# Which tiles a Strassen down-projection leaves plain, when its residuals are loaded, and in which order two 64x64 merges are issued

## The chip, the core and the metric

The kernel runs on one core of a Trainium2 chip, as one program. The metric is the device time of one execution in microseconds (us). The median of the runs is what a kernel is judged by. A separate profiled execution gives the trace from which the profile's lines come.

In the text PE is TensorE (matrix products), DVE is VectorE, ACT is ScalarE, POOL is GpSimd, and SP is SyncE, whose queue issues most of the transfers between the chip's main memory and the on-chip memory.

## The reference, cut to what matters

Two layers of a hybrid encoder over 1040 tokens (16 meta tokens and 1024 others), model width 1024, in float32. Each layer is a mixer followed by a SwiGLU block, with RMSNorm ahead of both and residual additions behind both. The mixer joins a bidirectional gated delta rule (4 heads of 128, chunks of 64) and a short gated convolution. What the change touches is this:

```python
# SwiGLU, D_FF = 2816 = 22 tiles of 128
gate, up = jnp.split(h @ w_gate_up, 2, axis=-1)
h = h + (jax.nn.silu(gate) * up) @ w_down
# gated delta rule, in each chunk and direction: a unit triangular system
A = M + jnp.eye(CHUNK)            # M strictly triangular
u = triangular_solve(A, vb); w = triangular_solve(A, kb * jnp.exp(G)[..., None])
```

The kernel works the chunks in blocks of 128 tokens and needs the inverse of one 128x128 unit triangular matrix for each block, head and direction: 8 blocks and 4 heads, 32 inverses a direction (a ninth block of 16 meta tokens is handled by itself).

## The kernel before

Activations lie transposed: 128 channels on the partitions, the tokens along the free dimension. Every float32 operand of a large product is split into a high part `hi`, rounded to the format that PE multiplies fast, and a remainder `lo`, and a product is three matmuls: hi by hi, hi by lo, lo by hi. The split is one ACT instruction (`hi`) and one DVE or POOL instruction (`lo`).

The program is written with a tile framework. It tracks dependencies between tiles, and at build time it places the instructions of each engine into one fixed order by priority and by a simulated timeline; on the chip each engine, and SP's queue of loads, then works through its list in that order. A helper `after(ins, prev)` adds a dependency by hand, `low(f)` issues PE work at the priority of the dense products, and three lists `jobs`, `jobs2`, `jobs3` hold small pieces of work: after each dense group (the products of one output tile over a third of the tokens or so) `dense` takes one piece from each list.

**The inverses.** `invert(d)` returns, for direction d, a list of steps that goes into `jobs3`, one step between two dense groups. A 128x128 inverse is put together from four 32x32 inverses, which DVE has worked out by substitution. `first`, `second` and `third` (lines 560, 568, 578) join 32x32 blocks into 64x64 ones. Then come the two products that join the two 64x64 halves, F_ and S_: `fourth` (line 589) multiplies a block of P_ (rows F_, columns S_) with X64 (rows F_) and puts the result, negated by ACT, into X64 (rows S_); `fifth` (line 594) multiplies that with P_ (rows S_) and puts the result into P_ (rows F_, columns S_). In each direction both are done for 32 matrices in four groups of eight, numbered by `qh`. The steps are `fourth` for groups 0 and 1, `fifth` for 0 and 1, `fourth` for 2 and 3, `fifth` for 2 and 3: four steps of 16 matmuls. The direction d = 0 uses two PSUM banks of the tag "f", d = 1 two of the tag "b". After the inverses of both directions comes the scan over the chunks, which runs between the remaining dense groups.

**Gate and up.** A loop over the 22 f tiles computes both projections by a Strassen scheme of seven products and ends with the row `uv = silu(gate) * up` of that tile, which SP writes to the scratch array `ad[f]` in main memory (line 1335). For some f, DVE also forms the difference of the row's two token halves (line 1337), which goes to the scratch array `td`.

**Down.** The down projection contracts over the 22 f tiles. Four of them (NF = 4) are taken plainly; the other 18 go through a Strassen scheme with seven products, in the order P2, P5, P3, P1, P6, P7, P4 (`SEVEN`). The 18 tiles form two halves `fh` of NP = 9 tiles, the output's 8 tiles two halves `dh` of 4, and the tokens two halves `z`: z = 0 is the two middle quarters, z = 1 the outer two. `UNITS` lists 84 units (product, block b of three tiles, output tile m): 12 units a product. A unit's matmuls (lines 1401 to 1403) are 18 of 260 columns in layer 0 and 9 of 512 columns in layer 1. Ahead of each unit the list `under[u]` issues what later units need:

- `w_unit(u + 5)`: the weight slice of the unit five further on, loaded by `a_load` or taken from sums of slices (`s_sum`), and split (lines 1181, 1182);
- `t_pair(t)`: the row for the right-hand operand, three for a block. It is loaded from `ad` by `b_load` (line 1200) or from `td` (line 1215) and split (lines 1223, 1224). P2 and P3 read the second half of the tiles (`fh` = 1), P1 and P7 the first;
- from unit 60 on, `plain_row`: the rows of the four plain tiles.

In the blocks b = 1 of P2, P5, P3 and P7 the loop also loads the residual half (`hd` to `hr`, line 1382) to which the product of this output tile is added at the end of its block b = 2, four units later. `hr` lies where two operands of gate and up were. The first slices and rows are issued while the last f tile is still being worked on (`down_begins`). After the units the four plain tiles are multiplied by an ordinary `dense`; in layer 1 their weights are split earlier (`last_weights`).

The plain tiles are f = 0 to 3, and the halves are f = 4 to 12 and 13 to 21:

```python
f0 = NF + NP * fh + 3 * (n // 4)                                        # a_load
dma(to.rearrange("p (g e) -> p g e", g=2), half(ad[NF + NP * fh + i][:, o0:L], z))   # b_load
if NF <= f < NF + NP:                                                    # gate and up
    ...
    dma(td[f - NF], gv[:, 0:NB])
```

Of the kernel before, what the change touches and what calls it, by code (L numbers as in the profile page):

```python
# [10 lines left out]
AF = mybir.ActivationFunctionType  # L11
# [6 lines left out]
L = 1040  # L18
H = 4
HD = 128  # L20
FT = 22
# [16 lines left out]
NF = 4  # L38
# [4 lines left out]
def trunk(ctx: ExitStack, tc: tile.TileContext, xT, w_in, w_ba, w_out, w_gu, w_dn,  # L43
# [235 lines left out]
    for l in range(DEPTH):  # L279
# [257 lines left out]
        def invert(d):  # L537
# [46 lines left out]

            F_, S_ = (slice(0, 64), slice(64, 128)) if d == 0 else (slice(64, 128), slice(0, 64))

            def fourth(qh):
                ps = fb(64)
                low(lambda: [mm(ps[S_, q, :], P_[F_, 8 * qh + q, S_], X64[F_, 8 * qh + q, :], start=True, stop=True) for q in range(8)])
                act(out=X64[S_, 8 * qh:8 * qh + 8, :], in_=ps[S_], func=AF.Copy, scale=-1.0)  # L590

            def fifth(qh):
                ps = fb(64)
                low(lambda: [mm(ps[F_, q, :], X64[S_, 8 * qh + q, :], P_[S_, 8 * qh + q, S_], start=True, stop=True) for q in range(8)])
                act(out=P_[F_, 8 * qh:8 * qh + 8, S_], in_=ps[F_], func=AF.Copy)

            return [first, second, third] + [lambda f=f, q=q: [f(q), f(q + 1)] for q in (0, 2) for f in (fourth, fifth)]

        l2s = {}

# [516 lines left out]
            return big(tag, dt).rearrange("p a b -> p (a b)")  # L1117

        def a_load(to, dh, fh, n):
            f0 = NF + NP * fh + 3 * (n // 4)  # L1120
            dma(to.rearrange("p (k e) -> p k e", k=3), w_dn[l, 4 * dh + n % 4, :, f0:f0 + 3, :])
            return to

# [73 lines left out]

        def b_load(fh, z, i):
            to = b_room()
            dma(to.rearrange("p (g e) -> p g e", g=2), half(ad[NF + NP * fh + i][:, o0:L], z))  # L1200
            return to

        def t_slot(t):
# [53 lines left out]
        for f in range(FT):  # L1257
# [75 lines left out]
            act(out=gv, in_=gv, func=AF.Silu)  # L1333
            tt(out=uv, in0=uv, in1=gv, op=ALU.mult)
            dma(ad[f][:, o0:L], uv)
            if NF <= f < NF + NP:
                tt(out=gv[:, 0:NB].rearrange("p (g e) -> p g e", g=2), in0=half(uv, 1), in1=half(uv, 0), op=ALU.subtract)
                dma(td[f - NF], gv[:, 0:NB])
            s_under(f)


# [6 lines left out]
        def plain_row(f):  # L1348

            u = b_room(2)  # L1350
            dma(u, ad[f][:, o0:L])
            lo = row(X[1], F32R, 3) if f < 3 else row(X[1] + "f", F32R)
            act(out=ax[:, f, o0:L], in_=u, func=AF.Copy)
            tt(out=lo[:, o0:L], in0=u, in1=ax[:, f, o0:L].bitcast(F32), op=ALU.subtract)
            rest.append((ax[:, f, :], lo))
# [5 lines left out]
        def last_weights(m):  # L1361
            if not fin_w:
                fin_w.append(flat(Y[0][2], F32R)[:, 0:4096].rearrange("p (m k e) -> p m k e", m=8, k=4))
                rows = [row(Y[1], F32R, 3) for _ in range(3)] + [row(Y[1] + "f", F32R)]
                fin_w.append([r[:, 512 * q:512 * q + 512].rearrange("p (k e) -> p k e", k=4) for r in rows for q in range(2)])
            hi, lo = fin_w[0][:, m], fin_w[1][m]
            wsplit(w_dn[l, m, :, 0:NF, :], hi, lo, raw4(("raw", "ck2")[m % 2]))
            wds.append([(hi[:, k], lo[:, k]) for k in range(4)])


# [2 lines left out]

        FIRST = {"P2": (0, 0), "P5": (1, 1), "P3": (0, 1), "P7": (1, 0)}
        bks = {}
        for i in range(NF):
            under[60 + 3 * i].append(lambda i=i: plain_row(i))
        for u, (p, b, m) in enumerate(UNITS):
            if b == 1 and p in FIRST:
                dh, z = FIRST[p]  # L1380
                q = 4 * dh + m
                dma(half(hr[q][:, o0:L], z), half(hd[q][:, o0:L], z))
            for fn in under[u]:
                fn()
            if last and u == 77:
                for q in range(KT):
                    last_weights(q)
            if not last and u >= len(UNITS) - 2:
                pre["dn", u - len(UNITS) + 2] = wload(w_dn[l, u - len(UNITS) + 2, :, 0:NF, :], NF)
            if p in ("P2", "P5", "P1") and b == 0:  # L1390
                for j in range(NJ):
                    bks[m, j] = pbank()
# [1 line left out]
            for j in range(NJ):  # L1394
                ps = bks[m, j]
                cs = slice(CW * j, CW * j + CW)
                for k in range(3):
                    th, tl = t_slot(3 * (u // 4) + k)
                    st = p in ("P2", "P5", "P1") and b == 0 and k == 0
                    en = b == NBK - 1 and k == 2  # L1400
                    mm(ps[:, :CW], wh[:, k, :], th[:, cs], start=st, stop=False, skip_group_check=True)  # L1401
                    mm(ps[:, :CW], wh[:, k, :], tl[:, cs], start=False, stop=False, skip_group_check=True)  # L1402
                    mm(ps[:, :CW], wl[:, k, :], th[:, cs], start=False, stop=en, skip_group_check=True)  # L1403
                if b == NBK - 1:
                    dh, z, op = TO[p]
                    h = part(hr[4 * dh + m], z, j)
                    tt(out=h, in0=pin(ps), in1=h, op=op)
# [4 lines left out]
        if not last:  # L1412
            for m in range(KT):
                then = next_norm(m, x[m], par[:, (l + 1) * P_L + P_N1 + m:(l + 1) * P_L + P_N1 + m + 1], ss)
                dense(pre.pop(("dn", m)) if m < 2 else wload(w_dn[l, m, :, 0:NF, :], NF), rest, chunks, add_h(m, then), pwide)
                dma(hd[m], hr[m])
        else:
            for (n0, n1) in FIN:
# [85 lines left out]
```

## Time and profile before

| What | Value |
|---|---|
| median of 3 runs | 2575.36 us (2570.45 to 2576.59) |
| the profiled execution | 2574.08 us, of which the trace's span is 2572.3 us |
| mean granted TensorE clock | 0.987 |
| PE busy | 2493.8 us, 97% of the span |
| DVE, ACT, POOL busy | 1722.1, 1046.3, 246.3 us |
| moved by DMA | 359.99 MB, mean 140 GB/s |
| Units of Down in layer 0, first to last start | 1073.3 to 1266.2 us |
| Units of Down in layer 1, first to last start | 2322.3 to 2506.7 us |
| merges (lines 589, 594) in layer 0, first to last start | 245.8 to 264.5 us and 318.5 to 338.4 us |
| merges in layer 1, first to last start | 1540.0 to 1559.6 us and 1616.7 to 1636.6 us |

Times in the trace are us from the span's start. "PE pf<-P,whi" is PE writing a PSUM tile of the tag "f" from operands in the tiles named P and whi; a tile's name here is that of its memory slot, so one slot serves many arrays over the run. A line "A <- B: 10.1, 1, 10.1" in the list of waits says that A stood idle until B, for 10.1 us in all, once, at most 10.1 us. In a timeline the columns are start, duration, engine, line, operation, tiles, shape and count, and in brackets the idle time ahead and what ended it. A matmul's duration overlaps the next one's: the pace is the distance between starts. A line of windows gives the window, its length, the busy time of PE, its weight loads, DVE, ACT and POOL (number of instructions in brackets), the granted clock, and the DMA engines' share and rate in GB/s.

### The profile page before, as it was taken

The page shows a single profiled execution, that of the slowest core. Times are in us where ns is not written, and L with a number is a line of the kernel's source. Part 1 is how long each engine was busy: PE and PEld are TensorE (multiplying, and loading weights), DVE is VectorE, ACT ScalarE, POOL GpSimd, SP SyncE. Part 2 cuts the span into 40 slices and gives each one's busy share as a digit, 9 for nine tenths or more (in the row PEclk, how much of TensorE's full clock was granted, in tenths as well). Part 3 has the DMA queues.
Part 4 walks back from the last instruction along what each step waited for, and adds up shares of the span by engine and source line. Part 5 has one row for each costly group of instructions (what it writes and reads, how often), then busy time and mean ns, then how long its engine had stood idle before and what let it go on. Part 6 is the DMA issues. An engine that isn't in the chain of part 4 may idle for free.

```text
span 2572.3 us, 44715 instructions
## 1 busy us (share of the span) xinstructions
PE 2493.8 (97%) x17442; PEld 2285.1 (89%) x17442; DVE 1722.1 (67%) x3055; ACT 1046.3 (41%) x1933; POOL 246.3 (10%) x264
## 2 busy tenths in 40 slices
PE   8989999999999999989999989999999999999997
PEld 6989999999999999989998878999888888887786
DVE  4678523549877777778656785235698767768866
ACT  5564323426333333434445633323453333334444
POOL 2041212200000000000011302222000000000002
PEclk9999999999999999999999999999999999999998
DMA  3458355524432222663323573456344222238431
GB/s 124 125 166 269 117 174 165 180 73 148 145 110 90 90 93 79 234 208 119 93 93 125 184 243 126 139 178 208 105 143 145 97 94 90 86 108 300 150 114 66
DMA packets 213567, 359.99 MB, mean 140 GB/s; under 512 B 25268, under 2 KB 87676, under 8 KB 213356
## 3 DMA queue, kind: packets, MB, share of 16 engines
q1 hardware_dynamic: 180684, 310.69, 36.8%
q10 hardware_dynamic: 30496, 42.09, 5.1%
q0 software_dynamic: 2176, 4.36, 0.6%
q8 instruction: 137, 2.24, 0.4%
q14 instruction: 74, 0.61, 0.1%
HBM read 266.60 MB, written 90.46 MB: 139 GB/s over the span
## 4 chain that ended last, share of the span: by engine, by line
PE 76%; DVE 9%; DMA 8%; issue 2%; ACT 2%; POOL 1%; ACTq 0%; SPq 0%; POOLq 0%; DVEq 0%
PE pacc L156 7%; PE pacc L158 7%; PE pacc L157 7%; PE pacc L1063 4%; PE pacc L1061 4%; PE pacc L1062 4%; PE pb L1063 3%; PE pb L1061 3%; PE pb L1062 3%; PE pf L1061 3%; PE pf L1063 3%; PE pf L1062 3%; PE pacc L1401 2%; PE pacc L1403 2%; PE pacc L1402 2%
## 5 line engine op out<-in xcount | busy, mean ns | idle before, releaser
L156 PE MATMUL pacc<-a,whi 128*128 128x346 f32 (+1 forms) x808 | 266.0, 332 | 14.2 <-ACT whi L129 9.6
L158 PE MATMUL pacc<-a,wlo 128*128 128x346 f32 (+1 forms) x808 | 266.4, 331 | 0.7 <-POOL wlo L130 0.7
L130 POOL TENSOR_TENSOR wlo<-raw,whi 128x512 fp32r<-128x512 f32 x92 | 123.1, 1340 | 1427.3 <-ACT whi L129 1357.1
L156 PE MATMUL pacc<-b,whi 128*128 128x346 f32 (+2 forms) x672 | 235.2, 351 | 0.5 <-DVE a L730 0.5
L158 PE MATMUL pacc<-b,wlo 128*128 128x346 f32 (+2 forms) x672 | 232.5, 348 | 1.0 <-DVE wlo L130 1.0
L157 PE MATMUL pacc<-a,whi 128*128 128x346 f32 (+1 forms) x688 | 227.0, 330 | 1.7 <-DVE a L900 1.7
L129 ACT ACTIVATE whi<-raw 128x512 fp32r<-128x512 f32 x168 | 105.2, 629 | 251.1 <-PE pacc L157 191.0
L157 PE MATMUL pacc<-b,whi 128*128 128x346 f32 (+2 forms) x580 | 201.5, 347 | 0.3 <-DVE b L900 0.3
L156 PEld LDWEIGHTS pacc<-a,whi 128*128 128x128 f32 x808 | 154.6, 192 | 19.8 <-ACT whi L129 10.7
L158 PEld LDWEIGHTS pacc<-a,wlo 128*128 128x128 f32 x808 | 155.8, 193 | 3.0 <-issue 1.5
L158 PEld LDWEIGHTS pacc<-b,wlo 128*128 128x128 f32 x672 | 126.9, 189 | 11.1 <-DVE wlo L130 1.3
L156 PEld LDWEIGHTS pacc<-b,whi 128*128 128x128 f32 x672 | 127.1, 189 | 10.4 <-issue 2.2
L157 PEld LDWEIGHTS pacc<-a,whi 128*128 128x128 f32 x688 | 132.0, 192 | 4.7 <-DVE a L900 2.0
L157 PEld LDWEIGHTS pacc<-b,whi 128*128 128x128 f32 x580 | 109.7, 189 | 8.8 <-issue 1.3
L1043 ACT ACTIVATE whi<-rw 128x512 fp32r<-128x512 f32 x92 | 58.1, 631 | 128.6 <-DVE rw L1271 29.8
L1043 ACT ACTIVATE b<-rw 128x512 fp32r<-128x512 f32 x64 | 40.2, 632 | 143.7 <-PE pacc L1062 47.3
L295 DVE TENSOR_TENSOR a<-pacc,rstd 128x346 f32<-128x346 f32 (+2 forms) x59 | 32.6, 553 | 83.7 <-PE pacc L158 83.6
L1426 POOL TENSOR_TENSOR b<-b,rstd 128x256 f32<-128x256 f32 (+1 forms) x12 | 13.3, 1137 | 726.2 <-DVE rstd L198 726.2
L1043 ACT ACTIVATE a<-rw 128x512 fp32r<-128x512 f32 x64 | 40.2, 629 | 101.6 <-PE pacc L1062 72.2
L295 DVE TENSOR_TENSOR b<-pacc,rstd 128x346 f32<-128x346 f32 (+1 forms) x63 | 32.2, 512 | 70.8 <-PE pacc L158 70.7
L1044 DVE TENSOR_TENSOR wlo<-rw,whi 128x512 fp32r<-128x512 f32 x92 | 62.9, 685 | 6.3 <-ACT whi L1043 5.6
L130 DVE TENSOR_TENSOR wlo<-raw,whi 128x512 fp32r<-128x512 f32 x76 | 52.3, 688 | 15.8 <-ACT whi L129 15.2
(969 smaller groups left out, 8041.7 us busy)
## 6 DMA issues: line engine op xcount, KB each, us to landing
raw<-in_w_in SPq DMA_DIRECT2D x112, 256.0 KB
raw<-in_w_gu SPq DMA_DIRECT2D x104, 256.0 KB
rw<-in_w_gu SPq DMA_DIRECT2D x88, 256.0 KB
rec<-aqd SPq DMA_DIRECT2D x62, 256.0 KB
rec<-vkd SPq DMA_DIRECT2D x61, 256.0 KB
rw<-in_w_dn SPq DMA_DIRECT2D x70, 192.0 KB
raw<-in_w_out SPq DMA_DIRECT2D x48, 256.0 KB
b<-ad SPq DMA_DIRECT2D x45, 260.0 KB
```

The costliest lines, as they stand in the source:

```text
L129: act(out=hi, in_=raw[:, 0:kk, :], func=AF.Copy)
L130: (tt if lov[0] else ptt)(out=lo, in0=raw[:, 0:kk, :], in1=hi.bitcast(F32), op=ALU.subtract)
L156: mm(ps[:, :n], wh, xh[:, n0:n1], start=(k == 0), stop=False)
L157: mm(ps[:, :n], wh, xl[:, n0:n1], start=False, stop=False)
L158: mm(ps[:, :n], wl, xh[:, n0:n1], start=False, stop=(k == K - 1))
L295: tt(out=t[:, n0:n1], in0=ps, in1=rstd[:, n0:n1], op=ALU.mult)
L1043: act(out=hi, in_=src, func=AF.Copy)
L1044: tt(out=lo, in0=src, in1=hi.bitcast(F32), op=ALU.subtract)
L1061: mm(ps[:, :CW], w[0][:, k, :], th[:, cs], start=first and k == 0, stop=False, skip_group_check=True)
L1062: mm(ps[:, :CW], w[0][:, k, :], tl[:, cs], start=False, stop=False, skip_group_check=True)
L1063: mm(ps[:, :CW], w[1][:, k, :], th[:, cs], start=False, stop=stop and k == nk - 1, skip_group_check=True)
L1401: mm(ps[:, :CW], wh[:, k, :], th[:, cs], start=st, stop=False, skip_group_check=True)
```

## The change

Three edits.

1. The plain tiles of Down become f = 18 to 21, and the two Strassen halves f = 0 to 8 and 9 to 17. `td` is formed in the f tiles 0 to 8. The scheme, the number of products and of loads stay as they are.
2. Each residual load is made to wait for the last matmul of the unit ahead of it (`unit_end`). Before, it had no such dependency.
3. `fourth` and `fifth` become one function `merges(a, b)`, which does `fourth` for group a and `fifth` for group b in one step and issues their matmuls in turn, one of each. The steps are (0, none), (1, 0), (2, 1), (3, 2), (none, 3): five instead of four.

```diff
--- before.py
+++ after.py
@@ -584,17 +584,25 @@
 
             F_, S_ = (slice(0, 64), slice(64, 128)) if d == 0 else (slice(64, 128), slice(0, 64))
 
-            def fourth(qh):
-                ps = fb(64)
-                low(lambda: [mm(ps[S_, q, :], P_[F_, 8 * qh + q, S_], X64[F_, 8 * qh + q, :], start=True, stop=True) for q in range(8)])
-                act(out=X64[S_, 8 * qh:8 * qh + 8, :], in_=ps[S_], func=AF.Copy, scale=-1.0)
-
-            def fifth(qh):
-                ps = fb(64)
-                low(lambda: [mm(ps[F_, q, :], X64[S_, 8 * qh + q, :], P_[S_, 8 * qh + q, S_], start=True, stop=True) for q in range(8)])
-                act(out=P_[F_, 8 * qh:8 * qh + 8, S_], in_=ps[F_], func=AF.Copy)
-
-            return [first, second, third] + [lambda f=f, q=q: [f(q), f(q + 1)] for q in (0, 2) for f in (fourth, fifth)]
+            def merges(a, b):
+
+                pa_, pb_ = (fb(64) if q is not None else None for q in (a, b))
+
+                def products():
+                    for q in range(8):
+                        if a is not None:
+                            mm(pa_[S_, q, :], P_[F_, 8 * a + q, S_], X64[F_, 8 * a + q, :], start=True, stop=True)
+                        if b is not None:
+                            mm(pb_[F_, q, :], X64[S_, 8 * b + q, :], P_[S_, 8 * b + q, S_], start=True, stop=True)
+
+                low(products)
+                if a is not None:
+                    act(out=X64[S_, 8 * a:8 * a + 8, :], in_=pa_[S_], func=AF.Copy, scale=-1.0)
+                if b is not None:
+                    act(out=P_[F_, 8 * b:8 * b + 8, S_], in_=pb_[F_], func=AF.Copy)
+
+            steps = [(0, None), (1, 0), (2, 1), (3, 2), (None, 3)]
+            return [first, second, third] + [lambda a=a, b=b: merges(a, b) for a, b in steps]
 
         l2s = {}
 
@@ -1117,7 +1125,7 @@
             return big(tag, dt).rearrange("p a b -> p (a b)")
 
         def a_load(to, dh, fh, n):
-            f0 = NF + NP * fh + 3 * (n // 4)
+            f0 = NP * fh + 3 * (n // 4)
             dma(to.rearrange("p (k e) -> p k e", k=3), w_dn[l, 4 * dh + n % 4, :, f0:f0 + 3, :])
             return to
 
@@ -1197,7 +1205,7 @@
 
         def b_load(fh, z, i):
             to = b_room()
-            dma(to.rearrange("p (g e) -> p g e", g=2), half(ad[NF + NP * fh + i][:, o0:L], z))
+            dma(to.rearrange("p (g e) -> p g e", g=2), half(ad[NP * fh + i][:, o0:L], z))
             return to
 
         def t_slot(t):
@@ -1333,9 +1341,9 @@
             act(out=gv, in_=gv, func=AF.Silu)
             tt(out=uv, in0=uv, in1=gv, op=ALU.mult)
             dma(ad[f][:, o0:L], uv)
-            if NF <= f < NF + NP:
+            if f < NP:
                 tt(out=gv[:, 0:NB].rearrange("p (g e) -> p g e", g=2), in0=half(uv, 1), in1=half(uv, 0), op=ALU.subtract)
-                dma(td[f - NF], gv[:, 0:NB])
+                dma(td[f], gv[:, 0:NB])
             s_under(f)
 
 
@@ -1348,7 +1356,7 @@
         def plain_row(f):
 
             u = b_room(2)
-            dma(u, ad[f][:, o0:L])
+            dma(u, ad[2 * NP + f][:, o0:L])
             lo = row(X[1], F32R, 3) if f < 3 else row(X[1] + "f", F32R)
             act(out=ax[:, f, o0:L], in_=u, func=AF.Copy)
             tt(out=lo[:, o0:L], in0=u, in1=ax[:, f, o0:L].bitcast(F32), op=ALU.subtract)
@@ -1364,7 +1372,7 @@
                 rows = [row(Y[1], F32R, 3) for _ in range(3)] + [row(Y[1] + "f", F32R)]
                 fin_w.append([r[:, 512 * q:512 * q + 512].rearrange("p (k e) -> p k e", k=4) for r in rows for q in range(2)])
             hi, lo = fin_w[0][:, m], fin_w[1][m]
-            wsplit(w_dn[l, m, :, 0:NF, :], hi, lo, raw4(("raw", "ck2")[m % 2]))
+            wsplit(w_dn[l, m, :, 2 * NP:FT, :], hi, lo, raw4(("raw", "ck2")[m % 2]))
             wds.append([(hi[:, k], lo[:, k]) for k in range(4)])
 
 
@@ -1373,20 +1381,21 @@
 
         FIRST = {"P2": (0, 0), "P5": (1, 1), "P3": (0, 1), "P7": (1, 0)}
         bks = {}
+        unit_end = None
         for i in range(NF):
             under[60 + 3 * i].append(lambda i=i: plain_row(i))
         for u, (p, b, m) in enumerate(UNITS):
             if b == 1 and p in FIRST:
                 dh, z = FIRST[p]
                 q = 4 * dh + m
-                dma(half(hr[q][:, o0:L], z), half(hd[q][:, o0:L], z))
+                after(dma(half(hr[q][:, o0:L], z), half(hd[q][:, o0:L], z)), unit_end)
             for fn in under[u]:
                 fn()
             if last and u == 77:
                 for q in range(KT):
                     last_weights(q)
             if not last and u >= len(UNITS) - 2:
-                pre["dn", u - len(UNITS) + 2] = wload(w_dn[l, u - len(UNITS) + 2, :, 0:NF, :], NF)
+                pre["dn", u - len(UNITS) + 2] = wload(w_dn[l, u - len(UNITS) + 2, :, 2 * NP:FT, :], NF)
             if p in ("P2", "P5", "P1") and b == 0:
                 for j in range(NJ):
                     bks[m, j] = pbank()
@@ -1400,7 +1409,7 @@
                     en = b == NBK - 1 and k == 2
                     mm(ps[:, :CW], wh[:, k, :], th[:, cs], start=st, stop=False, skip_group_check=True)
                     mm(ps[:, :CW], wh[:, k, :], tl[:, cs], start=False, stop=False, skip_group_check=True)
-                    mm(ps[:, :CW], wl[:, k, :], th[:, cs], start=False, stop=en, skip_group_check=True)
+                    unit_end = mm(ps[:, :CW], wl[:, k, :], th[:, cs], start=False, stop=en, skip_group_check=True)
                 if b == NBK - 1:
                     dh, z, op = TO[p]
                     h = part(hr[4 * dh + m], z, j)
@@ -1412,7 +1421,7 @@
         if not last:
             for m in range(KT):
                 then = next_norm(m, x[m], par[:, (l + 1) * P_L + P_N1 + m:(l + 1) * P_L + P_N1 + m + 1], ss)
-                dense(pre.pop(("dn", m)) if m < 2 else wload(w_dn[l, m, :, 0:NF, :], NF), rest, chunks, add_h(m, then), pwide)
+                dense(pre.pop(("dn", m)) if m < 2 else wload(w_dn[l, m, :, 2 * NP:FT, :], NF), rest, chunks, add_h(m, then), pwide)
                 dma(hd[m], hr[m])
         else:
             for (n0, n1) in FIN:
```

## The prediction

> **What bounds the kernel now.** I began with the page's head.
>
> ```profile
> span 2572.3 us, 44715 instructions
> PE 2493.8 (97%) x17442; PEld 2285.1 (89%) x17442; DVE 1722.1 (67%) x3055; ACT 1046.3 (41%) x1933; POOL 246.3 (10%) x264
> ```
>
> TensorE (PE) is busy 2493.8 of 2572.3 us. An edit can win in two ways only: by taking PE work away, or by closing one of PE's own gaps. So the second view was PE's waits by releaser.
>
> ```profile
> PE pf L1401 <- ACT P L1223: 10.1, 1, 10.1
> PE pacc L1403 <- DVE a L1182: 2.0, 1, 2.0
> PE pacc L156 <- DVE b L730: 1.9, 1, 1.9
> PE pacc L156 <- DVE a L730: 0.5, 1, 0.5
> ```
>
> The columns are total, times, longest. One wait stands out: a single 10.1 us ahead of a Down matmul (L1401), ended by ACT's split of a Down operand (L1223). The other three matter below. Third, PE's timeline around the 10.1 us:
>
> ```profile
> 1096.17 0.28 PE L1403 MATMUL pacc<-P,b 128*128 128x260 f32 x1
> 1106.52 0.59 PE L1401 MATMUL pf<-P,whi 128*128 128x260 f32 x1 [10.06 <-ACT P L1223]
> ...
> 1110.51 0.28 PE L1402 MATMUL pacc<-P,b 128*128 128x260 f32 x1
> 1110.63 0.28 PE L1403 MATMUL pacc<-P,b 128*128 128x260 f32 x1
> ```
>
> PE stops after 1096.17 and starts again at 1106.52. The eighteen matmuls that start from there up to 1110.51 take 3.99 us; the next two start 0.12 us apart, at which pace eighteen would take 2.16 us. The restart is slow, and that costs another 1.8 us. The stop is worth 10.1 + 1.8 = 11.9 us.
>
> Fourth, what was late: the SyncE queue (SP), which issues the loads in order, ACT's record and the chain that ended last.
>
> ```profile
> 1078.25 5.38 SPq L1382 DMA_DIRECT2D a<-hd  x8
> ...
> 1086.40 0.33 SPq L1335 DMA_DIRECT2D ad<-a  x1
> ...
> 1093.05 5.79 SPq L1382 DMA_DIRECT2D a<-hd  x8
> 1098.93 1.54 SPq L1121 DMA_DIRECT2D a<-in_w_dn  x3
> 1100.90 0.33 SPq L1200 DMA_DIRECT2D b<-ad  x1
> ```
>
> ```profile
> 1100.90 4.91 DMA b<-ad
> ```
>
> ```profile
> 1105.83 0.64 ACT L1223 ACTIVATE P<-b 128x520 fp32r<-128x520 f32 x1 [8.53 <-DMA b<-ad]
> ```
>
> SP writes the last f tile's row to `ad` at 1086.40. Reading it back goes out only at 1100.90, lands 4.91 us later, and ACT splits it at 1105.83. A unit of Down in layer 0 is 18 matmuls, 2.16 us. The first twelve units (product P2) need the B rows i = 0 to 8 of the second half, which are f tiles 13 to 21; PE stops inside units 8 to 11, which need i = 6, 7, 8. So it stops for f = 21, the tile that gate/up finished last. Between write and read back stand eight residual loads (`a<-hd`, 1093.05, 5.79 us of SP's time), and eight more went out at 1078.25. They are only added at the end of a product, some of them many units later.
>
> ```profile
> a<-hd SPq DMA_DIRECT2D x16, 260.0 KB
> ```
>
> ```profile
> 1070.00:1080.00 10.00, 10.00 (x85) 10.00 (x85) 7.35 (x11) 4.17 (x9) 0.00 (x0) 1.00 1.06 387
> 1080.00:1090.00 10.00, 10.00 (x86) 10.00 (x85) 6.81 (x13) 3.52 (x7) 0.00 (x0) 1.00 1.07 373
> 1090.00:1100.00 10.00, 6.46 (x54) 6.24 (x53) 7.76 (x14) 3.27 (x6) 0.00 (x0) 1.00 1.07 366
> 1100.00:1110.00 10.00, 3.48 (x16) 3.48 (x17) 3.58 (x7) 1.16 (x2) 0.00 (x0) 0.51 0.74 249
> ```
>
> The last two columns are the DMA engines' share and GB/s. From 1080 to 1100 the engines are full at 366 to 373 GB/s; the sixteen residual halves, 16 x 260 KB = 4.26 MB, are 11.4 us of transfer at 373.
>
> **Part 1: which tiles are plain.** Nothing is added or removed. P2 now reads f = 9 to 17, all written long before, and 18 to 21 become the plain rows, loaded from unit 60 on. The read back of a fresh row leaves P2, and with it the cause of the 11.9 us. What comes next is the bandwidth: from 1070 to 1110 the rows give 38.7 + 37.3 + 36.6 + 24.9 = 137.5, that is 13.75 MB. Without the sixteen residual loads and with the four that P2 still needs there (1.06 MB) it is 10.55 MB, 28.3 us at 373 GB/s; the time that is left without the stop is 40 - 11.9 = 28.1 us. These are level, and part of those bytes is wanted only later, so I take 0.9 us of stop as left: a gain of 11.0 us, ends 6 and 11.9.
>
> The `td` differences move from f = 4 to 12 to f = 0 to 8, in each layer.
>
> ```profile
> L1337 DVE TENSOR_TENSOR a3f<-a x5: 686/692/696, 744.4 to 900.4; 128x520 f32<-128x520 f32 x5
> ```
>
> ```profile
> 680.00:700.00 20.00, 20.00 (x167) 19.87 (x166) 18.02 (x33) 6.99 (x10) 0.00 (x0) 1.00 0.48 147
> ```
>
> Four subtractions of 0.69 us, each with its DMA on SP, move to tiles 0 to 3. There VectorE (DVE) has 18.0 of 20 us taken and PE none idle: the 2 us free per 20 us cover 0.69 us per tile. Cost 0; with no cover 4 x 0.69 = 2.8 us a layer. The plain rows' loads and weights are as many as before, at the same units.
>
> **Part 2: residual halves one unit ahead.** Each residual load now waits for the end of the unit before, in the b = 1 pass of P2, P5, P3 and P7: four waits a pass on SP. Queued behind a waiting load on SP are the weight slices (issued five units ahead), B rows (three to five units) and the sums' loads; ACT and DVE wait for those, and PE for them. From the start of its unit to its own use lie five units, 5 x 2.16 = 10.8 us, against 4.91 us to land: the residual itself is in time. A slice behind the wait has the same five units less landing (4.91) and split (ACT 0.64, DVE taken as the same), so 4.6 us are left. Cost 0 on that; the other end is rival C. What it frees is counted in part 1.
>
> Layer 1 has the same two bursts, and later DVE is full while PE waits for it (2.0 us, L1403, in the waits above):
>
> ```profile
> 2344.27 4.22 SPq L1382 DMA_DIRECT2D b<-hd  x8
> ```
>
> ```profile
> 2360.00:2370.00 10.00, 8.04 (x35) 6.18 (x34) 10.00 (x21) 3.31 (x7) 0.00 (x0) 1.00 0.71 215
> ```
>
> PE has 8.04 of 10 us there and DVE all 10: sums and splits arrive in a heap after the burst. With the burst spread out I take 1.6 of the 2.0 us; ends 0 and 2.0.
>
> **Part 3: the two 64x64 merges in turn.** Today each direction runs `fourth` on two quarters, then `fifth` on them, twice: four steps of 16 matmuls, each step between two dense groups. The new list has five: quarter 0's first product alone, three steps with eight of each kind in turn, and the last alone. Matmuls are equal in number, 64 a direction.
>
> ```profile
> 233.67 2.21 PE L568 MATMUL pf<-P,b 32*32 32x32 f32 x128
> ...
> 240.17 2.21 PE L578 MATMUL pf<-b,P 32*32 32x32 f32 x64
> ...
> 245.60 0.32 PE L156 MATMUL pacc<-a,whi 128*128 128x346 f32 x1
> 245.85 2.07 PE L589 MATMUL pf<-b,P 64*64 64x64 f32 x32
> 247.89 0.41 PE L157 MATMUL pacc<-a,whi 128*128 128x346 f32 x1
> ```
>
> ```profile
> L589 PE MATMUL pf<-b,P x64: 218/218/267, 245.8 to 259.1; 64*64 64x64 f32 x64
> ```
>
> A step is 32 records, two for each of 16 matmuls, in 2.07 us; a record lasts 0.22 us (L589 has 64 a direction for 32 matmuls), so starts are (2.07 - 0.22) / 31 = 0.060 us apart. From the dense matmul at 245.60 to the next at 247.89 are 2.29 us; less a dense matmul's own 0.16 (0.12 x 346 / 260), a step costs 2.13 us, of which 0.21 is entry and exit. Does taking turns help? `second` (L568) alternates two matmuls on disjoint rows and columns and does 128 records in 2.21 us; `third` (L578), same shape, one block only, does 64 in 2.21. Alternating halves the time. The 64x64 products use lower rows with upper columns and the reverse, disjoint in the same way. So a mixed step of 32 records costs 32 x 0.030 + 0.21 = 1.17 us and a lone one of 16 records 16 x 0.060 + 0.21 = 1.17 us: five are 5.85 us against 4 x 2.13 = 8.52. That is 2.67 us a direction, 10.7 us in four.
>
> [...]
>
> Not all of it arrives. In both layers PE waits for DVE soon after the first direction's merges (1.9 us and 0.5 us, L730). In layer 0 DVE is in the other direction's work:
>
> ```profile
> 279.39 2.23 DVE L544 STREAM_TRANSPOSE b<-x 128x1024 f32<-128x1024 f32 x1
> ...
> 285.34 0.94 DVE L730 TENSOR_TENSOR b<-pacc,b 128x346 f32<-128x346 f32 x2
> ```
>
> Transposes, independent of the merges, hold the eviction back until 285.34. PE arriving 2.67 us earlier would wait up to 2.67 us longer. The first direction thus gives between 0 and 2.67 us a layer; I take half. Merges: 2 x 2.67 + 2 x 1.33 = 8.0 us, ends 5.3 and 10.7. The fifth step puts the last merge one dense group later (24 x 0.16 = 3.8 us) and so the scan behind it; PE has dense groups to do meanwhile, so 0, at worst 3.8 us in a layer.
>
> **Sum.** 11.0 + 1.6 + 8.0 = 20.6 us. The profiled execution took 2574.1 us (span 2572.3 and 1.8 around it): 2553.5. The median of the runs, 2575.4, is 1.3 above it: 2554.8 us.
>
> **Rivals.**
> A. The transfers bind: the stop moves from the read back to the loads behind it (sums, `td`). For: the two sides, 28.3 and 28.1 us, are level. Against: part of the bytes is prefetch. Half of 11.9 stays: 2575.4 - 6 - 0.8 - 8.0 = 2560.6.
> B. Turns save nothing at 64x64 and the fifth step adds its 0.21 us four times: 2575.4 - 11.0 - 1.6 + 0.8 = 2563.6. Against: L568 beside L578. [...]
> C. Slower: SP held at the new waits. Place: the b = 1 passes. If the order on SP puts behind a wait loads whose unit is next, not five off, PE waits landing plus splits less one unit, 4.91 + 2 x 0.64 - 2.16 = 4.0 us; it decides once a needed load stands less than three units ahead (6.2 us is 2.9 units). Once a pass, eight passes: 32 us more, 2575.4 - 20.6 + 32 = 2586.8. For: SP is in order, its order is fixed beforehand, and it issued the last row at 1100.90 behind things not yet needed. Against: loads wait mostly for buffers, and those come free earlier than five units off.
> D. It does not do what it says: the queue, not the fresh row, was late. P2's last row is read late again or the next product's first; merges give only the second directions: 2575.4 - 5.3 = 2570.1.
>
> **Chances.** Forecast 0.58, A 0.14, B 0.11, C 0.08, D 0.09. This kernel's measurement tells about 0.3%, 7.7 us, from no change; below 2567.7 lie the forecast, A and B: faster 0.83; D is the same, 0.09; C slower, 0.08. The forecast's own range, from the ends of its terms, is 2575.4 - (11.9 + 2.0 + 10.7) = 2550.8 to 2575.4 - (6 + 0 + 5.3) = 2564.1. A and B lie inside it; the scan's 3.8 us in part (2.9) take the upper end to 2567.0; the runs shown reach 4.9 us below their median (2570.45), half of which I allow at the lower end: 2548.3 to 2567.0, which leaves C and D out, 0.17.
>
> **What would show it.** In the changed profile: no wait of over 3 us ahead of L1401 in layer 0's Down, and no slow matmuls after it; `hd` loads in four groups of single issues, each after a unit, not in two bursts of eight; DMA below its ceiling from 1080 to 1100; mixed steps of 32 records in about 1.2 us; PE's wait for L730 in layer 0 grown from 1.9 us by up to 2.67. Wrong, if PE's waits list a Down wait on a weight split or on `td` of several us (A or C), or if a mixed step still takes 2 us (B).

## The result, and the profile after

The changed kernel took 2552.79 us in the median of 5 runs (2551.66 to 2556.69), 22.6 us less than before: a ratio of 0.992, 95% interval 0.9907 to 0.9933. The forecast was 2554.8 us. The profiled execution also took 2552.79 us; the head of its page:

```profile
span 2551.0 us, 44782 instructions
PE 2486.7 (97%) x17442; PEld 2277.2 (89%) x17442; DVE 1721.1 (67%) x3055; ACT 1048.4 (41%) x1933; POOL 247.0 (10%) x264
```

PE has as many instructions as before, is busy 7.1 us less, and the span is 21.3 us shorter. Where the 21.3 us lie follows from cutting both traces at PE's first (for the units also last) matmul of a stage:

| stretch, us | before | after | difference |
|---|---|---|---|
| start to the first merge | 245.85 | 244.41 | -1.4 |
| layer 0: first merge to the first matmul of gate and up | 376.05 | 369.19 | -6.9 |
| gate and up | 451.40 | 451.50 | +0.1 |
| layer 0: units of Down | 192.87 | 180.78 | -12.1 |
| plain tiles, and layer 1 to its first merge | 273.87 | 275.92 | +2.1 |
| layer 1: first merge to gate and up | 352.56 | 351.27 | -1.3 |
| gate and up | 429.75 | 430.94 | +1.2 |
| layer 1: units of Down | 184.40 | 181.02 | -3.4 |
| plain tiles and end | 65.56 | 65.98 | +0.4 |

The rows outside Down's units and the stretches with the merges differ by 0.1 to 2.1 us, in both directions; so much is not explained by any edit.

**Down.** PE's waits (total, times, longest) now have no row from Down's matmuls, lines 1410 to 1412; the longest are others, and of the four rows shown of before the last two are left, now with L738:

```profile
PE pacc L156 <- ACT whi L129: 9.3, 3, 6.0
PE pb L489 <- DVE dt L499: 8.5, 3, 5.7
...
PE pacc L156 <- DVE b L738: 1.6, 1, 1.6
...
PE pacc L156 <- DVE a L738: 0.4, 1, 0.4
```

SP's timeline around the start of Down, which now lies at 1065.1 us instead of 1073.3:

```profile
1075.99 0.33 SPq L1343 DMA_DIRECT2D ad<-a  x1
...
1079.12 0.33 SPq L1391 DMA_DIRECT2D a<-hd  x1
...
1081.45 0.81 SPq L1391 DMA_DIRECT2D a<-hd  x2
...
1082.97 0.32 SPq L1391 DMA_DIRECT2D a<-hd  x1
...
1099.77 0.38 SPq L1391 DMA_DIRECT2D a<-hd  x1
...
1101.92 0.38 SPq L1391 DMA_DIRECT2D a<-hd  x1
...
1104.07 0.38 SPq L1391 DMA_DIRECT2D a<-hd  x1
```

The eight residual halves of a burst are gone: four loads close together, because SP comes to them late (the units that they wait for were over between 1073.7 and 1080.2 us, at 2.16 us a unit), then single ones 2.15 us apart, one a unit. The windows from three microseconds before Down's start on (last two columns: the DMA engines' share and GB/s):

```profile
1062.00:1072.00 10.00, 10.00 (x86) 10.00 (x85) 8.39 (x13) 4.40 (x9) 0.00 (x0) 1.00 1.05 380
1072.00:1082.00 10.00, 10.00 (x86) 10.00 (x85) 7.61 (x14) 4.02 (x9) 0.00 (x0) 1.00 1.06 362
1082.00:1092.00 10.00, 10.00 (x86) 10.00 (x85) 9.50 (x21) 5.08 (x11) 0.00 (x0) 1.00 0.64 218
1092.00:1102.00 10.00, 10.00 (x86) 10.00 (x86) 10.00 (x21) 4.38 (x10) 0.00 (x0) 1.00 0.63 186
```

PE is busy 10 of 10 us in all four. The DMA engines are as full as in the kernel before for the first twenty (shares of 1.05 and 1.06) and then at 64%: there was room.

**The merges.** PE's timeline, first a mixed step of the second direction, between two dense matmuls (L158, L156):

```profile
322.30 0.32 PE L158 MATMUL pacc<-a,wlo 128*128 128x346 f32 x1
322.56 0.27 PE L594 MATMUL pb<-b,P 64*64 64x64 f32 x1
322.56 0.27 PE L596 MATMUL pb<-P,b 64*64 64x64 f32 x1
322.66 0.22 PE L594 MATMUL pb<-b,P 64*64 64x64 f32 x1
322.67 0.22 PE L596 MATMUL pb<-P,b 64*64 64x64 f32 x1
322.72 0.22 PE L594 MATMUL pb<-b,P 64*64 64x64 f32 x1
322.73 0.22 PE L596 MATMUL pb<-P,b 64*64 64x64 f32 x1
...
323.48 0.22 PE L594 MATMUL pb<-b,P 64*64 64x64 f32 x1
323.49 0.22 PE L596 MATMUL pb<-P,b 64*64 64x64 f32 x1
323.63 0.43 PE L156 MATMUL pacc<-a,whi 128*128 128x346 f32 x1
```

The two kinds start 0.01 us apart and the pairs 0.06: 32 records from 322.56 to 323.71, 1.15 us. The first direction looks otherwise:

```profile
249.81 1.14 PE L596 MATMUL pf<-P,b 64*64 64x64 f32 x16
250.88 1.16 PE L489 MATMUL pb<-b,b 128*128 128x128 f32 x8
251.97 1.14 PE L594 MATMUL pf<-b,P 64*64 64x64 f32 x16
```

Here the order fixed at build time has one kind, other work (L489), and then the other kind: nothing takes turns. The time that the merges take from PE, from the start of the matmul ahead of each step to that of the one behind it, less 0.16 us a step:

| us | before | after | five steps in blocks | turns enforced |
|---|---|---|---|---|
| layer 0, first direction | 8.37 | 8.92 | 8.92 | 5.83 |
| layer 0, second | 8.38 | 5.83 | 8.06 | 5.83 |
| layer 1, first | 9.13 | 8.30 | 8.88 | 6.09 |
| layer 1, second | 8.46 | 6.08 | 8.15 | 5.88 |
| sum | 34.34 | 29.13 | 34.01 | 23.63 |

The last two columns are experiments (e4_apart, e5_turn below). The change saves 5.2 us, nearly all of it in the second directions.

### The profile page after: what moved, and what is told of

Same layout as the page of the kernel before. It is cut to its first block, busy times and chain, and to the rows that moved or that the text cites. A ratio compares the mean times of both kernels' runs of the same rounds, so it can differ in the third digit from the quotient of the medians.

```text
span 2551.0 us, 44782 instructions
## 1 busy us (share of the span) xinstructions
PE 2486.7 (97%) x17442; PEld 2277.2 (89%) x17442; DVE 1721.1 (67%) x3055; ACT 1048.4 (41%) x1933; POOL 247.0 (10%) x264
## 4 chain that ended last, share of the span: by engine, by line
PE 78%; DVE 9%; DMA 6%; issue 2%; ACT 2%; POOL 0%; ACTq 0%; POOLq 0%; DVEq 0%; SPq 0%
PE pacc L156 7%; PE pacc L158 7%; PE pacc L157 7%; PE pacc L1069 4%; PE pacc L1071 4%; PE pacc L1070 4%; PE pf L1069 3%; PE pf L1071 3%; PE pf L1070 3%; PE pb L1071 3%; PE pb L1069 3%; PE pb L1070 3%; PE pacc L1412 2%; PE pacc L1410 2%; PE pacc L1411 2%
## 5 line engine op out<-in xcount | busy, mean ns | idle before, releaser
L156 PE MATMUL pacc<-a,whi 128*128 128x346 f32 (+1 forms) x808 | 264.1, 330 | 11.1 <-ACT whi L129 9.3
L158 PE MATMUL pacc<-a,wlo 128*128 128x346 f32 (+1 forms) x808 | 264.2, 329 | 1.9 <-POOL wlo L130 0.7
L156 PE MATMUL pacc<-b,whi 128*128 128x346 f32 (+2 forms) x672 | 235.1, 350 | 1.1 <-ACT b L907 0.7
L158 PE MATMUL pacc<-b,wlo 128*128 128x346 f32 (+2 forms) x672 | 233.7, 349 | 0.3 <-DVE wlo L130 0.3
L156 PEld LDWEIGHTS pacc<-a,whi 128*128 128x128 f32 x808 | 153.2, 190 | 16.2 <-ACT whi L129 10.1
L158 PEld LDWEIGHTS pacc<-a,wlo 128*128 128x128 f32 x808 | 153.5, 190 | 3.6 <-issue 1.3
L156 PEld LDWEIGHTS pacc<-b,whi 128*128 128x128 f32 x672 | 127.1, 189 | 11.4 <-issue 1.5
L158 PEld LDWEIGHTS pacc<-b,wlo 128*128 128x128 f32 x672 | 127.3, 190 | 10.3 <-issue 1.5
```

The source lines that it names most:

```text
L156: mm(ps[:, :n], wh, xh[:, n0:n1], start=(k == 0), stop=False)
L158: mm(ps[:, :n], wl, xh[:, n0:n1], start=False, stop=(k == K - 1))
```

## The experiments

Each kernel is compared with the kernel before, run beside it on the same chip. The median of the kernel before was 2573.2 us beside e1, e2, e3 and e6, 2574.7 beside e0, e4, e5 and e7, 2576.1 beside e8 and e9, and 2573.4 beside e10 and e11.

### The Down edits, one at a time

e1_plain: the kernel before with edit 1 alone.

```diff
-            f0 = NF + NP * fh + 3 * (n // 4)
+            f0 = NP * fh + 3 * (n // 4)
...
-            dma(u, ad[f][:, o0:L])
+            dma(u, ad[2 * NP + f][:, o0:L])
```

> Only the plain tiles move to the end; residual loads and merges as before. Theory F (the stop of 10.1 us is the wait for the freshly written row of f = 21): the wait ahead of L1401 in layer 0 and the slow restart are gone although the two bursts of residual loads are still there; 11 to 12 us less, about 2563.5 us; DVE's 2.0 us wait in layer 1 stays. Theory Q (the transfers' queue is what binds): a wait of 5 us or more remains in Down of layer 0, at the same place or at the next loads; under 6 us less, about 2570 us or more.

Measured: 2559.43 us, ratio 0.9942 (0.9927 to 0.9957), 13.7 us less. Units 180.79 us in layer 0 and 181.02 us in layer 1: the stop of layer 0 is gone, and so is the 2.0 us wait of layer 1, which I had put down to the bursts.

e2_paced: the kernel before with edit 2 alone.

```diff
-                dma(half(hr[q][:, o0:L], z), half(hd[q][:, o0:L], z))
+                after(dma(half(hr[q][:, o0:L], z), half(hd[q][:, o0:L], z)), unit_end)
```

> Only the residual loads wait for the unit before; plain tiles and merges as before. Theory F: P2 still needs the row of f = 21, written at 1086.4, so a stop stays, but the burst of 5.8 us that stood ahead of the read back is gone: the stop shrinks to 3 to 6 us, and layer 1's 2.0 us wait goes; 6 to 9 us less, about 2568 us. Theory Q: without the bursts the stop is gone altogether; 13 to 14 us less, about 2561.5 us. Theory C (SP held at the waits costs): new waits of PE in the b = 1 passes.

Measured: 2563.11 us, ratio 0.9958 (0.9943 to 0.9972), 10.1 us less. Its list of PE's waits from 1060 to 1300 us, whole, and SP's timeline:

```profile
PE pf L1402 <- ACT P L1223: 1.4, 1, 1.4
PE pf L1403 <- DVE P L1224: 0.8, 1, 0.8
```

```profile
1078.96 0.33 SPq L1335 DMA_DIRECT2D ad<-a  x1
...
1085.98 0.32 SPq L1200 DMA_DIRECT2D b<-ad  x1
```

The fresh row is still read, but its read back goes out 7.0 us after its write instead of 14.5 (1086.40 to 1100.90 before), and of the 10.1 us stop 2.2 are left, less than the 3 to 6 expected. Units 183.47 and 181.47 us: layer 1 gains 2.9 of its 3.4 us here too, and its 2.0 us wait is gone. The 2.2 us are no longer a late load. The fresh row has landed by 1091.0 us, and PE has other work up to a matmul that starts at 1091.55; but ACT's fixed list has two other splits ahead of this row's, and the first of them waits for PE to be done with an old operand:

```profile
1091.52 1.69 ACT L1223 ACTIVATE P<-b 128x520 fp32r<-128x520 f32 x3 [3.99 <-PE pacc L1404]
```

The row's split is the third, from 1092.59 to 1093.21 us. So in layer 0 the row came late through both together, a fresh row in P2 and a burst ahead of its read back (in before, SP could issue the read back at 1100.90 us only when a residual load of the burst had landed at 1100.88). Taking away the fresh row is worth 12.1 us there, taking away the burst 9.4, both together 12.1.

e6_unpaced: the changed kernel without edit 2.

```diff
-                after(dma(half(hr[q][:, o0:L], z), half(hd[q][:, o0:L], z)), unit_end)
+                dma(half(hr[q][:, o0:L], z), half(hd[q][:, o0:L], z))
```

> The changed kernel without the waits on the residual loads (plain tiles and merges kept). Theory F: the stop in layer 0 is gone by the plain tiles alone, so what the waits brought is layer 1's 2.0 and 0.4 us: about 2 to 3 us over the changed kernel, 2555.5 us. Theory Q: a stop of several us comes back in layer 0; 2560 us or more.

Measured: 2555.16 us, ratio 0.9925 (0.9911 to 0.994). Units 180.79 and 181.02 us, as in the changed kernel, with the bursts back on SP:

```profile
1072.90 5.35 SPq L1391 DMA_DIRECT2D a<-hd  x8
...
1089.19 5.27 SPq L1391 DMA_DIRECT2D a<-hd  x8
```

With no fresh row behind them the bursts cost nothing, and layer 1's wait does not come back either. Beside edit 1, edit 2 brings nothing that these runs can measure.

e7_late: the changed kernel with each residual load four units later, at the unit that uses it.

```diff
-            if b == 1 and p in FIRST:
+            if b == NBK - 1 and p in FIRST:
```

> The changed kernel with each residual load one block later, at its own unit (b = 2), still waiting for the end of the unit before. It then has 2.16 us until its product is done and lands about 4.9 us after issue. Theory: the addition is about 2.8 us late in each of eight passes, DVE waits in it with the splits behind it, and PE waits for the bank: 10 to 25 us over the changed kernel. Rival (the splits' lead of several units hides it, the residual load is off the path whatever its place): within 3 us of the changed kernel.

Measured: 2551.28 us, ratio 0.9906 (0.9891 to 0.9921); units 180.83 and 181.01 us. DVE's waits have two new rows, and PE feels neither:

```profile
DVE a L1416 <- DMA a<-hd: 2.6, 3, 1.5
...
DVE b L1416 <- DMA b<-hd: 2.0, 2, 1.3
```

The expected loss of over 10 us did not come: a residual load that is itself late costs PE nothing here. The run was built to make the residual late, not the loads queued behind SP's waits, so it tests rival C only in passing.

### The merges

e3_merge: the kernel before with edit 3 alone (the functions of the diff above).

> Only the merges. In the changed kernel's order of PE the second direction's mixed steps alternate, the first direction's mostly stand in blocks of one kind. Theory M (only alternating saves): 2.67 us less for each second direction, nothing for the first: 5.3 us less, about 2570 us; the 10.1 us stop stays. Rival (the time saved is lost to DVE or to the scan, which starts a dense group later): 0 to 2 us less. Rival (all four directions gain): 8 us or more less.

Measured: 2567.68 us, ratio 0.9982 (0.9971 to 0.9994), 5.5 us less. Both of Down's waits stay, so they are independent of the merges:

```profile
PE pf L1409 <- ACT P L1231: 9.4, 1, 9.4
...
PE pacc L1411 <- DVE a L1190: 2.0, 1, 2.0
```

e4_apart: the changed kernel, five steps as there, the two kinds in blocks.

```diff
-                    for q in range(8):
-                        if a is not None:
+                    if a is not None:
+                        for q in range(8):
                             mm(pa_[S_, q, :], ...)
-                        if b is not None:
+                    if b is not None:
+                        for q in range(8):
                             mm(pb_[F_, q, :], ...)
```

> The changed kernel with its five steps, but in each the eight matmuls of one kind and then the eight of the other. Theory M (alternating saves the time): mixed steps of the second direction take 2.1 us and not 1.15, three in each layer, so 5.3 us over the changed kernel before anything else; but the five steps, and with them the scan one dense group later, stay. Theory K (part of layer 0's gain is that the scan, one group later, does not fall into the half clock): layer 0 from the second direction's merges to the start of gate and up still takes 3 to 5 us less than before the change. If K is wrong, that stretch is as long as before the change, 303 us.

Measured: 2558.03 us, ratio 0.993 (0.9918 to 0.9943), 5.2 us over the changed kernel run beside it (e0_after); the two intervals overlap a little. PE's timeline of the step shown above:

```profile
324.36 0.97 PE L594 MATMUL pb<-b,P 64*64 64x64 f32 x13
325.12 0.27 PE L597 MATMUL pb<-P,b 64*64 64x64 f32 x1
...
325.34 0.92 PE L597 MATMUL pb<-P,b 64*64 64x64 f32 x13
```

Except for three pairs at the seam the kinds follow each other, and the step takes 1.9 instead of 1.15 us. The merges' sum is 34.01 us, 4.9 over the changed kernel, whose saving was 5.2: nearly all of the saving of PE time comes from the turns.

e5_turn: the changed kernel, the first matmul of each kind in a mixed step held until both evictions of the step before are done.

```diff
+            ends = [None, None]
...
+                    held = list(ends) if a is not None and b is not None else []
...
+                            one = mm(...)
+                            for e in (held if q == 0 else ()):
+                                after(one, e)
...
+                    ends[0] = act(...)
```

> The changed kernel with one more dependency: the first matmul of each kind in a mixed step waits for both evictions of the step before, so that both kinds stand ready together and all twelve mixed steps alternate, also the first direction's. PE has about 4.6 us less to do (five more steps at 1.0 us less, less some waiting). If DVE does not take it back: 3 to 4 us under the changed kernel. If it does (my forecast's lower end, a longer wait for the eviction L738): within 1 us of it.

Measured: 2548.11 us (2546.52 to 2551.35), ratio 0.9897 (0.9884 to 0.9911); e0_after beside it 2552.86 (2550.0 to 2555.73). All twelve mixed steps take turns and the merges' sum falls to 23.63 us. The gain of the profile lies in layer 1, whose stretch from the first merge to gate and up is 346.18 us against 351.61 in e0_after. Layer 0's is 371.37 against 370.83: it has 10.2 us at half clock against 3.4, and a longer wait for DVE behind the first direction (1.7 us in e0_after):

```profile
PE pacc L156 <- DVE b L745: 3.1, 1, 3.1
```

e0_after: the changed kernel itself.

> The changed kernel itself, beside the next three on the same chip: about 2553 us, 0.992 of the kernel before. In layer 0 no wait ahead of L1409, no half clock in the scan (10.2 us of it before).

Measured: 2552.86 us, ratio 0.9914 (0.9901 to 0.9928). Its scan in layer 0 has 3.4 us at half clock, where none was expected.

### Where the scan falls

Layer 0's stretch from the first merge to gate and up fell by 6.9 us in the profile, and only 2.0 of that are merges (0.55 more, 2.55 less). Windows of before, around two waits in its scan, then of after; the granted clock stands ahead of the last two columns:

```profile
510.00:520.00 10.00, 5.93 (x23) 5.14 (x24) 9.98 (x15) 6.55 (x19) 2.92 (x2) 0.65 1.02 394
520.00:530.00 10.00, 10.00 (x63) 9.53 (x62) 5.82 (x18) 1.99 (x7) 1.28 (x1) 0.83 0.17 63
```

```profile
500.00:510.00 10.00, 6.58 (x48) 6.19 (x46) 6.17 (x11) 8.00 (x22) 4.97 (x3) 1.00 0.86 314
510.00:520.00 10.00, 9.47 (x69) 9.08 (x69) 9.48 (x24) 1.99 (x8) 0.63 (x1) 1.00 0.87 329
```

PE's waits there are as long after (2.1 and 1.9 us) as before (1.7 twice, 0.4 and 0.3), but before had 10.2 us at half clock with them, and after none. The loss is some 5 us by my estimate, from Down's matmuls, which start 0.22 us apart at half clock (1106.90 to 1110.15 us of before) and 0.12 at full. Is that difference the place of the scan, which five steps put one dense group later?

e8_gap: the kernel before, with one empty step ahead of the second direction's merges.

```diff
-                jobs3.extend(invert(1))
+                inv = invert(1)
+                jobs3.extend(inv[:3] + [None] + inv[3:])
```

> The kernel before with one empty step ahead of the second direction's four merge steps, in both layers: no matmul is added or removed and none takes turns, but those merges, and the scan behind them, come one dense group later. Theory K (the part of layer 0's gain that the turns do not explain comes from the scan being one dense group later, clear of the stretch at half clock): layer 0's stretch from the second direction's merges to the start of gate and up, 303.4 us before, falls by about 3.5 us to near 300, with no half clock in the scan; layer 1's stays within 1 us; the time falls by about 3 us to some 2571. Rival (the half clock of before was an accident of that profile, or the five steps themselves did it): the stretch stays at 302.5 to 303.5 and the time at 2574. The prediction's own bound: an empty step costs up to 3.8 us a layer, 2578 to 2582.

Measured: 2572.15 us, ratio 0.999 (0.998 to 1.0). Layer 0's stretch is 372.14 us, 4.0 under the 376.1 that the three kernels with the old merges average (before, e1_plain, e2_paced: 376.05, 375.16, 377.11), with 3.4 us at half clock instead of 10.2 in each of them. Layer 1's is 353.74, 1.2 over their 352.5. This trace agrees with the theory for layer 0, though not all of the half clock is gone; in the time the interval reaches no change. e4_apart agrees as well: with five steps and hardly any turns, layer 0 takes 299.9 us from the second direction's first merge to gate and up, against 303.4 before, with 3.4 us at half clock. e5_turn does not: its scan is as late and has the 10.2 us again. Each of these is one profile, and among the five profiles of the merges as changed layer 0's stretch has 0 to 6.8 us at half clock.

e9_gap2: the same empty step in the changed kernel.

> The changed kernel with the same empty step: the second direction's merges, still taking turns, and the scan come one more dense group later. Theory K, if later is better only as far as the slow stretch is left: layer 0's stretch stays near 296 us (measured 296.1 to 297.7 without the step) and the time at 2552.8 within 2 us. Rival (every group of delay helps the scan): a further 2 to 4 us, near 2550. Rival (the prediction's bound, the scan's end now being late): 2 to 4 us more a layer, 2556 to 2560.

Measured: 2548.99 us, ratio 0.9893 (0.9878 to 0.9908); stretches 366.89 and 350.02 us. PE's waits from 440 to 600 us are now one row, and no half clock is left there:

```profile
PE pacc L157 <- DVE a L909: 0.3, 1, 0.3
```

e11_gap3: two empty steps.

> The changed kernel with two empty steps ahead of the second direction's merges. Layer 0's waits in the scan are already down to 0.4 us with one empty step, so if those waits and the slow clock behind them are all there is to gain, the second step brings nothing: layer 0's stretch from the first merge to gate and up stays within 1 us of 366.9, the time within 2 us of 2549.0. Rival (the prediction's bound of 3.8 us a layer for a scan that is late): 369 to 371 us in layer 0 and 2552 to 2556. Rival (each group of delay goes on helping): 364 to 365 us and 2546.

Measured: 2549.39 us, ratio 0.9905 (0.9888 to 0.9922). Layer 0's stretch is back at 371.62 us, with 4.35 us of waits in the scan and 3.4 us at half clock; layer 1's is 349.21. In these profiles, then, a group of delay is neither a gain nor a loss as such: the scan meets other waits.

e10_both: e5_turn and e9_gap2 together.

> The changed kernel with both additions tried singly: every mixed step of the merges is forced to take turns (2548.1 us by itself), and one empty step stands ahead of the second direction's merges (2549.0 by itself). If the two gains are separate (one from shorter steps of the first direction and of layer 1's scan, one from the scan's place), they add: layer 0's stretch from the first merge to gate and up, 369 to 372 us in the changed kernel, falls to 365 or less, layer 1's, 351.3 to 351.6, to 345, and the time to 2544 to 2546. Rival: both gains are the scan's place against the dense groups, met by two roads; then they overlap and the time stays at 2547 to 2550.

Measured: 2546.42 us (2543.44 to 2547.87), ratio 0.9896 (0.9881 to 0.9911), 27.0 us under before; e5_turn alone was 26.6 and e9_gap2 27.2 under theirs. The gains do not add: the stretches are 367.11 and 347.90 us, the wait for DVE behind the first direction is 3.9 us against 2.3 in e9_gap2, and 3.4 us at half clock lie in the same part. All three are some 5 us under the changed kernel by medians; their intervals overlap its interval (0.9901 to 0.9928), and each other's. They are the best versions found, and which of them is best stays open.

## Why the prediction was right, and where its steps were not

**Part 1 (11.0 us): mechanism right, size 12.1.** No stop is left in layer 0's units. The stop was 10.1 us of wait and 2.0 of slow matmuls (192.87 - 180.78 - 10.06), where I had 1.8; the trace of before has the clock at half from 1100.2 to 1110.4 us, which covers them. The 0.9 us kept back for the bandwidth was not needed: the DMA engines are full for the first twenty microseconds only (shares of 1.05 and 1.06, then 0.64 and 0.63). That settles rival A. The differences `td` cost nothing that shows: the stretches of gate and up move by +0.1 and +1.2 us, within what untouched rows do.

**Part 2 (1.6 us): the effect came, the cause was half the truth.** Layer 1's units lost 3.4 us: waits of 2.0 and 0.4, the rest unnamed. Pacing alone does bring most of it (2.9 us in e2_paced), but e1_plain brings all of it without pacing, and e6_unpaced keeps it without pacing. The failed step is "sums and splits arrive in a heap after the burst", taken as the whole cause: with the tiles of edit 1 the burst costs nothing. The heap itself shows. From 30 to 40 us after layer 1's first unit DVE is busy 6.5 of 10 us in before and in e3_merge and has no pause in the ten that follow, in which PE waits for it; in e1_plain and e6_unpaced it is busy 9.0 us there, in e2_paced and in the changed kernel all 10. How the choice of tiles relieves DVE in layer 1 was not tried further. The zero for SP's waits held, and rival C with its 32 us found no support: no matmul of Down waits in the changed kernel.

**Rival D was half a truth.** I set the queue against the fresh row; e1_plain and e2_paced show that the row's lateness needed the two together. That is why D's consequence, a row late again, did not come. Its other half, that the merges give only in the second directions, did: 4.9 of the 5.2 us lie there.

**Part 3 (8.0 us): turns right, two terms mis-sized.** A mixed step in which all matmuls take turns costs 1.17 us by the table's measure, as forecast, and layer 0's second direction 5.83 us of PE (forecast 5.85, before 8.38): 2.55 and 2.38 us saved where I had 2.67. That removes rival B. In the mixed step shown of the profile after, two products on disjoint blocks start about 0.01 us apart, and only the pairs keep the 0.06 us.

The failed term is the first direction. I took half of 2.67 a layer, on the ground that DVE would eat the other half. It brought -0.55 and +0.83 us, because its mixed steps took turns nowhere in layer 0 and in one of three in layer 1; I had read the order off the source, and the order that counts is the one fixed at build time. DVE's wait did not grow (1.9 to 1.6 us). Where turns are enforced, my reasoning does appear: 3.09 us less of merges in layer 0 and 1.4 us more of that wait in e5_turn, and 1.6 more in e10_both than in e9_gap2, about half. These are single profiles, and with the merges as before or as changed that wait lies anywhere between 0.9 and 2.7 us, so "half" is rough.

The second mis-sized term is the scan's zero. Averaged over the five profiles with these merges (after, e0_after, e3_merge, e6_unpaced, e7_late), layer 0's stretch is 370.8 against 376.1 us. Of these 5.3 us, 2.0 are merges and 3.4 by the same estimate the half clock: half of the 6.8 us less of it (10.2 against 3.4 on average). Layer 1's stretch is 351.6 against 352.5, though its merges save 3.2 us: 2.3 us are given back, 0.9 of it as waits in the scan. So the scan gained 3.4 in one layer and lost 2.3 in the other; the bound of 3.8 held, and only the loss had been thought of. That its later place is the cause is likely for layer 0 but not shown, because e5_turn, with the same five steps, is back at 10.2 us of half clock.

**The sum.** 12.1 + 3.4 in Down and 8.2 in the two stretches, less 2.3 on the other rows, are the 21.3 us of the profiles. The forecast 20.6 came close because Down's excess of 2.9 us stands against 1.8 us too few in part 3 (5.3 + 0.9 = 6.2 on average), and the single profile has more of the scan's luck than the average.

## What to carry to other kernels

Here a row that was just written and a burst ahead of its read back in SP's list made one stop between them; look for both, and expect that the two cures do not add (12.1 and 9.4 us in layer 0's units, 12.1 together). When the load is in time, look at the place of its row in the next engine's list too (third of three in ACT's list in e2_paced, where PE still waited 2.2 us). An order written in the source is not yet the order on the engine: where small matmuls are to take turns, see that both kinds are ready together, and read the turns off the timeline (seven of twelve mixed steps took turns in the changed kernel). A piece of work that is moved by one step also moves what stands behind it, so price both ends of the move, a gain as well as a loss (the scan gained 3.4 us in one layer and lost 2.3 in the other).

## What was unexpected in the hardware

The half clock in layer 0's scan came with two waits of 1.7 us that lie 1.6 us of work apart, and stayed for 10.2 us (513.0 to 523.3 us in before); waits of 2.1 and 1.9 us in the changed kernel were met at full clock in one profile, and with 3.4 us at half clock 26 us behind them in the next (e0_after). In the traces of before and after, all stretches at half clock but the last of each trace last 3.41, 6.83, 10.24 or 17.07 us. The longest of PE's waits in before's scan was 1.7 us. Whether waits set off the half clock, and in which pattern, was not settled.
